# A decoder layer on one core: TensorE's order taken from the source instead of the scheduler, small products gathered into larger groups, and the first norm laid out by hand

## Chip, core and metric

The kernel runs on one core of one Trainium2 chip. The metric is the device time of one execution in microseconds (us), lower is better. The kernel before took 437.94 us, the median of 3 runs (437.6 to 438.55).

## What is computed

One decoder layer for 256 tokens of width 1024 in float32. Cut to what matters:

```python
h = rms_norm(x, norm1_g)
z = h @ w_in                      # RWKV part | MoBA q, k, v | gates of two branches
a = rwkv7_time_mix(shift_mix(z_rwkv))     # 8 heads of 64, a state updated over 256 tokens
b = moba_attention(rope(qk_norm(q)), rope(qk_norm(k)), v)   # 8 heads; one block: causal softmax
m = sigmoid(g_a) * (a @ w_branch_a) + sigmoid(g_b) * (b @ w_branch_b)
x = x + m @ w_out
h = rms_norm(x, norm2_g)
u, g = h @ w_ffn_up               # 2816 channels each
y = x + (gelu(causal_conv3(u)) * g) @ w_ffn_down
```

The RWKV part computes for each head and token the recurrence `S = S * w + (S a) b^T + v k^T`, `y = S r`, then a norm for each head (group norm), a bonus term and a gate. The kernel computes it by 4 chunks of 64 tokens: inside a chunk all tokens are joined by a triangular 64x64 system, whose inverse is built up from 16x16 blocks; between chunks a 64x64 state is passed on.

## The kernel before

**Large products.** Every product with a weight matrix is made in three products of a rounded format, so that nearly float32 remains: both operands are split into a high and a low part, and hh·whi, hl·whi and hh·wlo are summed in PSUM. The weights stream in 125 tiles of 512 KB (128 partitions x 1024). `queue` lists them in the order of use; `load_next` (L228 to L235) issues the next one on SyncE's queue into one of 4 buffers `raw`; `split_hi` (L239) casts it into `whi` on ScalarE (L246; three tiles, the entries of `HI_ENG`, on VectorE); `split_lo` (L251) subtracts on VectorE (L256) and makes `wlo`, of which there are 3 buffers; then the next load is issued, so SyncE's place in the queue hangs on VectorE's. `weights` takes a ready pair and makes the next. `wst` (L273, products 128x256 at L284, L286, L289) and `xst` (L295, products 128x512 at L305, L306, L309) run through one output tile and give control back after each part of a tile.

**Threads.** Between the first projection and branch a, five generators share the engines: `bulk` (the projections k, r, v of RWKV, then q, k, v of MoBA, then 8 gates, then branch b), `chain` (RWKV's chain of small steps), `att` (attention), `gn` (the group norm of each chunk) and `lv1` (the second half of the inverse's upper levels). A thread that yields says what its step costs on TensorE and after what latency the results will be there:

```python
cost, lat = next(th[1])
now_t += cost
th[2] = now_t + lat * SLACK.get(th[0], 1.0)
```

A loop keeps a clock `now_t`, always takes the first thread in the list whose time has come, and stretches the latencies by `SLACK`. So it writes the source's order. The framework's scheduler then orders the instructions of each engine anew by its own estimates, TensorE among them; `tc.issue_after` ties a few places.

**RWKV's chain,** in order: the sigmoids of decay and `a` (L490 ff.); exponentials e2, e3 of the running decay; the norm of kk: sums by small products `pss`, `rq` = 1 / sqrt on VectorE, `rx` = its broadcast on ScalarE, transposed by TensorE (`prx`); then the operands AR and KB (L561 to L579; one KB part on GpSimd at L572, two on VectorE at L574, 64x1024 each). `pgr` (L592) multiplies KB and AR in four groups through two banks of PSUM into G (VectorE, L595). The diagonal 16x16 blocks of G go to DRAM `d1` and come back as `Tb` (SyncE, L602, L604). A solve of 15 steps, two VectorE instructions each (L612, L614), builds their inverses `Xb`, which go out to `d2` and come back as X (L617, L623). Beside this stand the transposes KBt (L634), VU (L647), Z0 (L658), and the bonus and gate products `ch` and `pg` (L675 to L677), read by VectorE at L679 and L685. Then `level` (L704 ff.) uses X: products `pp`, a mask P on VectorE (L708), products `px` and `py`, added into X, for the 16 and the 32 level, half by half. Then the 4 chunks pass one after another: pz, pu (copied into VU on ScalarE and VectorE), pS and py. After each, `group_norm` makes yc and its transposed products `pc`, then yah and yal.

**Attention** (L847 ff.): transposes of q and k, then for each of four quarters (token half, head half) scores `ps`, maximum, exp on ScalarE (L889), normalisation head by head on VectorE, transposes (`ppt`, copied to pT on ScalarE at L905), and the product with v (`po`, into ybh at L917 and ybl at L918).

**Head.** Four loads on SyncE's queue bring x, four more the first weight tiles; norm1_g comes on GpSimd's queue, ten parameter rows (p1) on SyncE's behind the first four weight tiles, the other small parameters on GpSimd's. `norm_t` makes the norm, the transposes and hh, hl (L357, L358) from it. ScalarE loads a function table when the kind of function changes.

**End.** `branch(0)`, then w_out in two halves (xst), after each the transposes `turned` (L1001) with hh (L1004) and hl (L1005) of half of the channels and the squares for the second norm; then 11 rounds of the FFN: `proj2` twice, a convolution and GELU, and `down` (L1043 to L1045) one round later. The token's scale of the second norm is applied after the first product (`token_scale`).

Each PSUM tile is one of three sorts: `acc` (3 banks, for large products), `ch` (3 banks, the chain) and `at` (2 banks, attention).

## Time and profile before

| | |
|---|---|
| median of 3 runs | 437.94 us |
| profiled execution | 438.61 us |
| its span | 436.8 us (1.8 us lie around it) |
| TensorE products, busy in the span | 425.6 us, 3600 instructions |
| VectorE | 301.4 us, 545 |
| ScalarE | 243.0 us, 391 |
| GpSimd | 12.8 us, 21 |
| data moved by DMA | 70.76 MB, mean 162 GB/s |

In the profile PE is TensorE (PEld its weight loads), DVE VectorE, ACT ScalarE, POOL GpSimd and SP SyncE. A group's row gives the line, the engine, the operation, output and inputs by the program's names with their sizes, the number of instructions, the busy time, the mean duration in ns, and the idle time of the engine just ahead with what ended it. A row of the timeline gives the start, the duration, and the same. The duration of a product is longer than the distance between two starts, as products are pipelined.

### The profile page before, as it was taken

What the parts mean: (1) busy time and instruction counts of PE and PEld (TensorE: products, weight loads), DVE (VectorE), ACT (ScalarE), POOL (GpSimd) and SP (SyncE); (2) the same over time, 40 slices, a digit from 0 to 9 for tenths busy, and PEclk for the clock granted to TensorE, in tenths of its full rate; (3) what the DMA queues carried; (4) which work ended last, traced back from release to release, by engine and by line L of the source; (5) the groups of instructions that cost most, each with busy time, mean ns of one, the idle gap of its engine ahead of it and who ended that gap; (6) DMA issues with size and microseconds to landing.
All of it is one profiled execution on the core that took longest, in us unless ns stands there. A gap on an engine that the chain in (4) does not pass through costs nothing.

```text
span 436.8 us, 8837 instructions
## 1 busy us (share of the span) xinstructions
PE 425.6 (97%) x3600; PEld 384.0 (88%) x3600; DVE 301.4 (69%) x545; ACT 243.0 (56%) x391; POOL 12.8 (3%) x21
## 2 busy tenths in 40 slices
PE   7799998999999999999999999999999999999996
PEld 3688996788899989799997899999999999999995
DVE  4695899698456568676796479576576576576573
ACT  6489852644375446777355378455455455465450
POOL 6000040000000000000000000000000000000000
PEclk9999999999999999999999999999999999999999
DMA  8764836543657331164556366655665656565612
GB/s 234 195 190 125 243 94 195 132 129 54 194 154 230 95 104 51 50 190 127 166 182 195 107 211 184 226 189 166 200 192 178 195 193 191 191 182 185 214 50 96
DMA packets 62189, 70.76 MB, mean 162 GB/s; under 512 B 8898, under 2 KB 52617, under 8 KB 62150
## 3 DMA queue, kind: packets, MB, share of 16 engines
q1 hardware_dynamic: 61750, 69.50, 53.1%
q0 software_dynamic: 400, 0.71, 0.6%
q8 instruction: 28, 0.46, 0.4%
q14 instruction: 11, 0.09, 0.1%
HBM read 68.76 MB, written 1.44 MB: 161 GB/s over the span
## 4 chain that ended last, share of the span: by engine, by line
PE 82%; DVE 5%; ACT 5%; DMA 4%; issue 1%; SPq 1%; DVEq 0%; ACTq 0%
PE acc L284 15%; PE acc L286 15%; PE acc L289 15%; PE acc L305 4%; PE f L1045 4%; PE f L1043 4%; PE f L1044 4%; PE acc L306 4%; PE acc L309 4%; DMA raw<-in_w_in_dram 4%; DVE wlo L256 2%; ACT whi L246 1%; PE ps L876 1%; PE pp L704 1%; PE py L720 1%
## 5 line engine op out<-in xcount | busy, mean ns | idle before, releaser
L246 ACT CAST whi<-raw 128x1024 fp32r<-128x1024 f32 x121 | 126.4, 1050 | 119.3 <-PE acc L286 52.6
L256 DVE TENSOR_TENSOR wlo<-raw,whi 128x1024 fp32r<-128x1024 f32 x125 | 152.2, 1219 | 53.1 <-PE acc L289 18.4
L284 PE MATMUL acc<-hh,whi 128*128 128x256 f32 x600 | 150.1, 284 | 1.7 <-ACT whi L246 0.8
L286 PE MATMUL acc<-hl,whi 128*128 128x256 f32 x600 | 148.7, 282 | 0.9 <-DVE hl L358 0.9
L284 PEld LDWEIGHTS acc<-hh,whi 128*128 128x128 f32 x600 | 113.1, 188 | 4.4 <-ACT hh L357 1.5
L286 PEld LDWEIGHTS acc<-hl,whi 128*128 128x128 f32 x600 | 113.1, 188 | 3.2 <-DVE hl L358 1.5
L289 PE MATMUL acc<-hh,wlo 128*128 128x256 f32 x600 | 95.1, 281 | 1.2 <-DVE wlo L256 1.2
L289 PEld LDWEIGHTS acc<-hh,wlo 128*128 128x128 f32 x600 | 80.9, 189 | 2.1 <-DVE wlo L256 2.0
L1044 PE MATMUL f<-whi,hb 128*128 128x512 f32 x80 | 31.1, 389 | 0.0
L1043 PE MATMUL f<-whi,hb 128*128 128x512 f32 x80 | 31.1, 389 | 0.0
L1045 PE MATMUL f<-wlo,hb 128*128 128x512 f32 x80 | 31.1, 389 | 0.0
L305 PE MATMUL acc<-whi,hh 128*128 128x512 f32 x48 | 20.2, 425 | 0.0
L306 PE MATMUL acc<-whi,hl 128*128 128x512 f32 x48 | 18.8, 393 | 0.0
L1058 DVE TENSOR_TENSOR an<-acc,rsb 128x512 f32<-128x512 f32 x11 | 7.6, 691 | 14.8 <-PE acc L289 13.9
L1045 PEld LDWEIGHTS f<-wlo,hb 128*128 128x128 f32 x80 | 15.0, 188 | 3.1
L1044 PEld LDWEIGHTS f<-whi,hb 128*128 128x128 f32 x80 | 15.0, 188 | 2.7
L1043 PEld LDWEIGHTS f<-whi,hb 128*128 128x128 f32 x80 | 15.0, 188 | 2.7
L1076 DVE TENSOR_TENSOR cv<-cv,acc 128x256 f32<-128x256 f32 x22 | 8.3, 418 | 11.5 <-PE acc L289 11.2
L309 PE MATMUL acc<-wlo,hh 128*128 128x512 f32 x48 | 15.0, 393 | 0.0
L1065 ACT ACTIVATE cv<-an,cpar 128x256 f32<-128x256 f32 x22 | 12.0, 594 | 1.4 <-DVE an L1058 0.4
L305 PE MATMUL acc<-whi,mh 128*128 128x512 f32 x32 | 12.8, 399 | 0.0
L306 PE MATMUL acc<-whi,ml 128*128 128x512 f32 x32 | 12.6, 395 | 0.0
(274 smaller groups left out, 566.1 us busy)
## 6 DMA issues: line engine op xcount, KB each, us to landing
raw<-in_w_ffn_up_dram SPq DMA_DIRECT2D x44, 512.0 KB
raw<-in_w_in_dram SPq DMA_DIRECT2D x43, 512.0 KB
raw<-in_w_ffn_down_dram SPq DMA_DIRECT2D x22, 512.0 KB
raw<-in_w_out_dram SPq DMA_DIRECT2D x8, 512.0 KB
x<-in_x_dram SPq DMA_DIRECT2D x8, 256.0 KB
raw<-in_w_branch_b_dram SPq DMA_DIRECT2D x4, 512.0 KB
raw<-in_w_branch_a_dram SPq DMA_DIRECT2D x4, 512.0 KB
out_dram<-o SPq DMA_DIRECT2D x3, 256.0 KB
```

Source lines behind the costliest of these rows:

```text
L246: act.copy(hi[:, :k * c], raw[:, :k * c])
L256: dve.tensor_tensor(lo[:, :n], raw[:, :n], hi[:, :n].bitcast(F32), op=OP.subtract)
L284: pe.matmul(om, wh[:, k, ms], xh[:, k0 + k], start=k0 + k + m == 0, stop=False, skip_group_check=True)
L286: pe.matmul(om, wh[:, k, ms], xl[:, k0 + k], start=False, stop=False, skip_group_check=True)
L289: pe.matmul(om, wl[:, k, ms], xh[:, k0 + k], start=False, stop=k0 + k == nk - 1 and m == n - 1, skip_group_check=True)
L305: pe.matmul(ps_[t], xh[:, K, ts], wh[:, k], start=K == 0, stop=False)
L306: pe.matmul(ps_[t], xl[:, K, ts], wh[:, k], start=False, stop=False)
L309: pe.matmul(ps_[t], xh[:, K, ts], wl[:, k], start=False, stop=K == nk - 1)
L1043: pe.matmul(fin[f], hb[:, 0, i, ts], wh[:, 0, cs], start=st, stop=False)
L1044: pe.matmul(fin[f], hb[:, 1, i, ts], wh[:, 0, cs], start=False, stop=False)
L1045: pe.matmul(fin[f], hb[:, 0, i, ts], wl[:, 0, cs], start=False, stop=False)
L1065: act.activation(cv, pm, AF.Identity, scale=cpar[:, 44 + n:45 + n], bias=cpar[:, 66 + n:67 + n])
```

## The change

- TensorE keeps the source's order (`tc.manual_schedule(engines={PE})`). `SLACK` is gone; the latencies that the threads give are longer, and the costs are set to 0.345 and 0.69 us for a k block. The wait ahead of the upper levels goes from 16.0 (times 1.7) to 11.0.
- Small products come in larger groups: L490 in one group of 8 instead of two, KBt in one and ahead of pgr, pgr in two groups instead of four, over four banks, VU and Z0 in one each, both halves of the upper levels together (`below`, `masked`, `onto`; the thread `lv1` is gone), scores of all eight heads for the first token half, the product with v by token half, normalisation in one multiplication.
- The first norm and the first product are written out in `first_steps`, in which the order of PE, ACT, DVE and POOL is the source's. The first wlo is made on GpSimd. norm1_g, rwkv_mu and the biases come on ScalarE's queue, all other small parameters on SyncE's behind the first four weight tiles; GpSimd loads nothing. The masks are made on GpSimd.
- `HI_ENG` is gone: all casts from the fourth tile on stand on ScalarE.
- q of MoBA is projected ahead of RWKV's v, k and v of MoBA between and after, with the first gate between them.
- At the second norm `turned(0, 4)` stands inside the second half of w_out, `turned(4, 8)` behind the first weight tile of the first FFN product, `token_scale` within the second product.

```diff
-SLACK = {"chain": 1.7, "att": 1.4, "lv1": 2.5, "gn": 2.0}
-        HI_ENG = {i: dve for i in (4, 5, 6)}
...
-        p0 = t1("p0", (8, 128))
-        nc.gpsimd.dma_start(p0, rows(norm1_g, 8))
         x_sb = load_x()
+        load_rows(act, p1, ((rows(norm1_g, 8), 8), (mu1[0:1792].rearrange("(n c) -> n c", c=128), 14),
+                            (mu1[1696:1824].rearrange("(n c) -> n c", c=128), 1),
+                            (rows(decay_bias, 4), 4), (rows(aaa_bias, 4), 4)))
...
         for _ in range(NRAW):
             load_next()
-        for dst, src in p1_loads:
-            nc.sync.dma_start(dst, src)
+        small_loads()
...
+        def first_steps():
...
+            split_hi(dve)
+            split_lo(pool)
+            for k in range(6):
+                parts(k)
+            split_hi(act)
+            parts(6)
+            parts(7)
+            split_lo()
+            split_hi(act)
+            p = acc()
...
+        with tc.manual_schedule(engines={E.PE, E.Activation, E.DVE, E.Pool}):
+            p = first_steps()
+        late_consts()
...
-            yield 0.5, 2.0
+            yield 1.5, 5.0
             dve.tensor_tensor(flat(kp), flat(kp), flat(zk), op=OP.mult)
...
+            yield 1.4, 4.0
+            masks()
+            for g in range(2):
+                pg = [[p.rearrange("p (u i) -> p u i", u=4) for p in pj] for pj in banks("pgr")]
+                for ct in (2 * g, 2 * g + 1):
...
+                yield 2.1, (5.0, 0.1)[g]
...
-                yield 2.6, 0.2
+                yield 2.7, 0.2
...
-            yield 0, 16.0
-            yield from level(0)
-            threads.insert(1, ["lv1", level(1), 0.0])
+            yield 0, 11.0
+            pp = [below(g) for g in range(2)]
+            P = [masked(pp[g], m16) for g in range(2)]
+            yield 2.5, 3.5
+            adds = [onto(0, P[0], 0), onto(1, P[1], 0), onto(0, P[0], 1)]
+            for a in adds:
+                a()
+            yield 3.3, 4.5
...
-                    yield 0, 1.0
+                    yield 0, 6.0
+                    while not joined[0] and "chain" not in done:
+                        yield 0, 0.1
                     p = chp("pc").rearrange("p (a n) -> p a n", a=8)
...
+            p0 = yield from scores(0, 0, 8)
+            yield weighted(0, p0)
+            pa = yield from scores(1, 0, 4)
+            pb = yield from scores(1, 1, 4)
+            yield weighted(1, pa + pb)
+            yield 0, 2.5
             ybs.extend((ybh, ybl))
...
+            rope_tables()
+            yield from attention_input(0)
+            yield from proj4("v", 8)
+            yield from attention_input(1)
+            yield from gates(1, 0)
+            yield from attention_input(2)
+            threads.insert(1, ["att", attention(), now_t + 3.0])
+            for j in range(1, 4):
+                yield from gates(1, j)
+            for j in range(4):
+                yield from gates(0, j)
             while "att" not in done:
                 yield 0, 1.0
             yield from branch(1, *ybs)
...
-                th[2] = now_t + lat * SLACK.get(th[0], 1.0)
+                th[2] = now_t + lat
+                if cost:
+                    joined[0] = th[0] != "bulk"
...
             if j == 0:
-                with tc.issue_after(mid[0]), tc.issue_after(mid[1]):
-                    pa = now(proj2())
-                    token_scale()
+                pa = acc()
+                gen = wst(pa, 2, hh, hl)
+                steps(gen, 2)
+                turned(4, 8)
+                squares(1, *WCUT[1:3])
+                run(gen)
                 fin = [chp("f0"), chp("f1"), chp("f2"), atp("f3")]
+                pb = acc()
+                gen = wst(pb, 2, hh, hl)
+                steps(gen, 2)
+                token_scale()
+                run(gen)
...
     with tile.TileContext(nc) as tc:
-        body(tc, *args)
+
+        with tc.manual_schedule(engines={mybir.EngineType.PE}):
+            body(tc, *args)
```

In the changed text `below(g)` makes the 16 products `pp` of one half, `masked` the mask's multiplication into P, and `onto(g, P, side)` 16 products onto one side of X with the addition handed back as a function; `scores(t, j, nh)` holds what attention did from `ps` to pT for `nh` heads, and `weighted(t, pTs)` the products `po` of one token half; `steps(gen, n)` runs n parts of a product; `squares` makes the sums for the second norm.

More of the change, by code (lines that the diff above doesn't have):

```diff
@@ L395, in body @@
             load_next()
-        for dst, src in p1_loads:
-            nc.sync.dma_start(dst, src)
-        hh, hl, xn, part, first, turn, second = norm_t(x_sb, G1, "1", (0, 512, 1024))
-        for t in range(2):
-            part(t, 0)
-            part(t, 1)
-            if t:
-                with tc.issue_after(last):
-                    last = dve.tensor_copy(par[:, 0:8], pt[:, 0:8]).ins
-                with tc.issue_after(last):
-                    last = first(t)
-            else:
-                last = first(t)
-            turn(t)
@@ L440, in now @@
                     return e.value
-        with tc.issue_after(mid[0]):
-            p = now(proj2())
         xwa = t1("xwa")
@@ new lines, in masked, with onto @@
+            def masked(p, mk):
+                P = b2("P", [128, 8, 64])
+                dve.tensor_tensor(P, p, mk[:, None, :].to_broadcast([128, 8, 64]), op=OP.mult)
+                return P
+            def onto(g, P, side):
+                p, p4 = bank("px")
+                for u, i in us[g]:
+                    for q in range(2):
+                        l, r = X[bsl(q), 1, u], P[bsl(q), i]
+                        if side:
+                            l, r = r, l
+                        pe.matmul(p[bsl(q), i], l, r, start=True, stop=True)
+                return lambda: dve.tensor_tensor(pair(X[:, side], g), pair(X[:, side], g), p4, op=OP.add)
@@ L729, in chain @@
+            yield 2.3, 4.0
             ny = {}
@@ L951, in bulk, with attention_input @@
             yield from proj4("r", 0)
-            yield from proj4("v", 8)
-            for i in range(3):
+            def attention_input(i):
                 qkv.append(b4("qkv", (128, 2, 8, 64)))
@@ L958, in bulk @@
                     finish_qk(ps_[t], i, t)
-            threads.insert(1, ["att", attention(), 0.0])
-            yield from gates(1)
-            yield from gates(0)
+            rope_tables()
[7 more added lines that the diff above has]
+                yield from gates(1, j)
+            for j in range(4):
+                yield from gates(0, j)
             while "att" not in done:
```

513 lines of the change are left out of this document (249 added, 264 removed).

## Prediction

> **What bounds the kernel now.** I read the page first, then the busy time by stretch, then TensorE's timeline around its gaps, then the groups by line.
>
> ```profile
> span 436.8 us, 8837 instructions
> PE 425.6 (97%) x3600; PEld 384.0 (88%) x3600; DVE 301.4 (69%) x545; ACT 243.0 (56%) x391; POOL 12.8 (3%) x21
> PEclk9999999999999999999999999999999999999999
> PE 82%; DVE 5%; ACT 5%; DMA 4%; issue 1%; SPq 1%; DVEq 0%; ACTq 0%
> L246 ACT CAST whi<-raw 128x1024 fp32r<-128x1024 f32 x121 | 126.4, 1050 | 119.3 <-PE acc L286 52.6
> L256 DVE TENSOR_TENSOR wlo<-raw,whi 128x1024 fp32r<-128x1024 f32 x125 | 152.2, 1219 | 53.1 <-PE acc L289 18.4
> ```
>
> TensorE is busy for 425.6 of 436.8 us at the full clock. DVE and ACT have room on the average, but each weight tile costs 1.05 us on ACT and 1.22 on DVE, and every short step of a chain queues behind such an instruction. By stretch (length, then busy time and instructions of PE, its weight loads, DVE, ACT, POOL; clock; DMA share; GB/s):
>
> ```profile
> 0.00:25.60 25.60, 20.25 (x115) 14.62 (x115) 15.98 (x63) 15.47 (x30) 7.84 (x19) 1.00 0.74 205
> 25.60:118.80 93.20, 91.28 (x731) 79.01 (x730) 74.97 (x153) 55.04 (x90) 5.00 (x2) 1.00 0.56 153
> 118.80:224.40 105.60, 105.56 (x1327) 97.51 (x1326) 72.68 (x135) 63.54 (x116) 0.00 (x0) 1.00 0.44 131
> ```
>
> TensorE's gaps are 5.35 us in the head, 1.92 in the second stretch, 0.04 in the third. So the change can win through the head, two stalls, and dead time inside "busy": a switch between large and small products.
>
> ```profile
> 142.56 0.63 PE L289 MATMUL acc<-hh,wlo 128*128 128x256 f32 x4
> 143.11 1.15 PE L704 MATMUL pp<-X,G 64*64 64x64 f32 x32
> 144.19 0.38 PE L284 MATMUL acc<-hh,whi 128*128 128x256 f32 x1
> 144.41 0.28 PE L286 MATMUL acc<-hl,whi 128*128 128x256 f32 x1
> 144.53 0.28 PE L284 MATMUL acc<-hh,whi 128*128 128x256 f32 x1
> ```
>
> The last two starts lie 0.12 apart, the pitch of large products. The fourth L289 starts near 142.91, so L704 comes 0.20 after it: 0.08 lost. The 32 small ones start every 0.03 ((1.15 - 0.22) / 31), the last near 144.04, and L284 follows 0.15 later: 0.12 lost. L286 comes 0.22 after that: 0.10 lost. One visit to small products costs **0.3 us**.
>
> **What is saved.** All large products stay (600 of 128x256 in each of three lines, and so on); I count the same 2496 in both orders. In the order of TensorE's instructions the small ones stand in 55 groups before and 34 after; without the head and the second norm it is 49 and 30. 19 visits x 0.3 = **5.7** (0.2 to 0.35 each: 3.8 to 6.7).
>
> ```profile
> 69.27 0.48 PE L592 MATMUL pgr<-AR,KB 64*128 64x128 f32 x2
> 70.86 1.16 PE L592 MATMUL pgr<-AR,KB 64*128 64x128 f32 x14 [1.10 <-DVE G L595]
> 41.38 0.38 PE L284 MATMUL acc<-hh,whi 128*128 128x256 f32 x1 [0.75 <-ACT whi L246]
> ```
>
> The products of pgr waited for a bank that DVE emptied. In the change they use four banks and come in groups of 32 with 5 us between: 70.86 - 69.27 less two pitches, **1.3**. The wait for a whi at 41.38 falls among groups that are now one: **0.8** (0 to 0.8; the three casts taken from DVE may bring it back, see below).
>
> The head:
>
> ```profile
> 13.68 1.05 ACT L246 CAST whi<-raw 128x1024 fp32r<-128x1024 f32 x1 [2.11 <-DMA raw<-in_w_in_dram]
> 7.60 2.30 SPq L397 DMA_DIRECT2D p<-in_rwkv_mu_dram  x2
> 15.48 0.25 SPq L397 DMA_DIRECT2D p<-in_rwkv_r_k_dram  x1
> 17.93 0.95 SPq L234 DMA_DIRECT2D raw<-in_w_in_dram  x2
> ```
>
> The second raw tile lands late, with POOL's loads beside it, and SP reaches the fifth only at 17.93, behind ten small loads. After, five of them stand on ACT's queue and none on POOL's; but 15 stand on SP behind the fourth raw, the tanh of xwa stands behind two more casts (2.1 us), and the first small group needs it. I take **1.6** saved; the bounds are the whole wait saved (2.1) and 4 lost (15 issues at 0.25 us, as at 15.48). POOL's first wlo lies under the eight hh casts. The masks on POOL (busy 5.00 us in the second stretch) hide under the chain's first products; uncovered they would cost a few tenths. Saved in all: 5.7 + 1.3 + 0.8 + 1.6 = **9.4**.
>
> **What is added.** TensorE now runs strictly as the source says: where the planner's latency is too short, it stands, and nothing can pass. The rows that price it:
>
> ```profile
> 85.38 0.46 SPq L604 DMA_DIRECT2D Tb<-d  x1
> ...
> 100.08 1.49 SPq L617 DMA_DIRECT2D d<-Xb  x2
> 104.02 4.04 SPq L623 DMA_DIRECT2D X<-d  x8
> ```
>
> ```profile
> 77.50 1.29 DVE L595 TENSOR_TENSOR G<-pgr,gmask 128x512 f32<-128x512 f32 x2 [0.99 <-PE pgr L592]
> ...
> 90.44 0.17 DVE L612 TENSOR_TENSOR tmp<-Tb,Xb 128x15 f32<-128x15 f32 x1
> ...
> 94.06 1.23 DVE L256 TENSOR_TENSOR wlo<-raw,whi 128x1024 fp32r<-128x1024 f32 x1 [0.29 <-PE acc L309]
> ...
> 95.86 0.68 DVE L679 TENSOR_TENSOR zr<-ch,zv 128x512 f32<-128x512 f32 x1
> ...
> 99.88 0.17 DVE L614 TENSOR_TENSOR Xb<-Xb,tmp 128x15 f32<-128x15 f32 x1
> ```
>
> ```profile
> 119.73 0.56 PE L704 MATMUL pp<-X,G 64*64 64x64 f32 x10
> ```
>
> ```profile
> L747 ACT ACT_TABLE_LOAD x4 | 5.1, 1283 | 0.1
> L931 ACT ACTIVATE gt<-acc 128x512 f32<-128x512 f32 x8 | 4.8, 594 | 0.1
> L889 ACT ACTIVATE sc<-sc,mx 128x128 f32<-128x128 f32 (+1 forms) x16 | 7.1, 444 | 3.7 <-DVE mx L886 3.7
> L574 DVE TENSOR_TENSOR KB<-kp,L 64x1024 f32<-64x1024 f32 x2 | 4.1, 2068 | 0.0
> L905 ACT COPY pT<-ppt 128x256 f32<-128x256 f32 (+1 forms) x8 | 3.8, 477 | 5.7 <-PE ppt L904 5.5
> L1005 DVE SCALAR_TENSOR_TENSOR hl<-xt,par,hh 128x256 fp32r<-128x256 f32 x8 | 3.5, 479 | 1.3 <-ACT hh L1004 1.3
> L1004 ACT ACTIVATE hh<-xt,par 128x256 fp32r<-128x256 f32 x8 | 3.4, 474 | 7.2 <-PE xt L1001 6.8 <-DVE hl L1005 0.4
> L917 ACT CAST ybh<-po 128x256 fp32r<-128x256 f32 x4 | 1.5, 370 | 2.6 <-PE po L913 2.6
> ```
>
> I went through the changed order of each engine with these durations.
> - The transposes prx need rx. On DVE the two KB products (2.07 each, L574 above) now stand ahead of rq. The planner leaves about 5 us; 4.1 of KB, one wlo and the steps of rq come to 6.3. With a late weight tile behind it: **1.7** (0.4 to 2.5).
> - The second group of ch and pg needs the bank that DVE empties into zr (L679 above). This instruction stands half way through the 30-step solve, which stands behind a wlo that waits for TensorE to free a buffer. In before G ends at 78.8, Tb is issued at 85.38 (6.6 later), the solve starts at 90.44 and zr at 95.86 (5.4 of solve, one wlo within). After, TensorE has 14.6 us of work between the G products and this group (54 large ones of both widths, 11.0, and three small groups, 3.6); DVE has 2.7 of G, then 6.6 to the issue, 3 to the landing (an estimate below the 5.06 from issue to first step in before), 5.4 of solve and at least 0.5 of MoBA's k norm between its steps: 18.2. So **3.6** (0 to 9).
> - The products pp need X. In before X's last issue ends at 108.1; with 1.3 for its landing, an estimate, that is 13.5 behind zr at 95.86, and L704 came only at 119.73: 10 us of room. After, TensorE has 13.7 of work from there (72 large ones, 12.4, and the group itself), and the stretch holds two wlo (2.4) and small steps of the norm more on DVE: **2.6** (0 to 6).
> - pS waits for VU, whose copy stands behind eight exps (0.44 each), a tanh and a cast on ACT: **0.9** (0 to 1.5).
> - The end of attention. In before it ended with 24 large products of the gates left. After, all are gone at the 888th, and then come the last group norm, the last transposes, 16 products po, and branch b, which needs ybh. The norm has a tanh (0.59), a whi (1.05), a table load (1.28) and a sqrt ahead on ACT, the multiplication of sc and a wlo (1.22) on DVE: about 5; then a copy pT (0.48), ybh (0.37) and its remainder: **6.4** (2.4 with nothing queued ahead, to 9).
> - The first FFN product: hh and hl of chunks 4 to 7 are now made after its first raw's products. The first pair takes 0.47 + 0.48, the others follow every 0.47 where the products need one every 0.23: 0.95 + 4 x 0.24 = 1.9, so **2.0** (0.5 to 3.5).
>
> Added in all: 1.7 + 3.6 + 2.6 + 0.9 + 6.4 + 2.0 = **17.2**. Three casts more on ACT (3 x 1.05) I cost at nothing: between 25.6 and 118.8 ACT is busy for 55.0 of 93.2; uncovered they cost 3.2.
>
> **The sum.** 17.2 - 9.4 = +7.8. The profiled execution took 438.61 (span 436.8 and 1.8 around it), so it would become 446.4; against the median of the runs shown, 0.67 lower, **445.7**. With every wait at its low end and the savings as above: 3.3 - 9.4 = -6.1; that end is the first rival.
>
> **The rivals.**
> - *Faster.* The chains do not queue behind casts as I laid them out: waits last only what a chain needs by itself. The solve is the place: if Tb lands early enough that zr and X come in time (0 in place of 6.2), pS 0, prx 0.4, attention's end 2.4, FFN 1.5, the waits are 4.3: 4.3 - 9.4 = -5.1, **432.8**. For it: the planner's latencies are longer and planned for this order, and in before all these chains had room. Against it: DVE's and ACT's order is fixed too, with wlo and whi between the steps. It decides where the waits sum to less than 9.4, 55% of what I found.
> [...]
> - *ACT bounds the second stretch* through the three casts: +3.2, **448.9**.
> - *Gains and waits cancel*: within 0.2%, about what a measurement of this kernel can tell from no change.
>
> **How the numbers follow.** Forecast, waits outweigh gains: 0.48 (its own range 440 to 450). Faster: 0.30 (430 to 437). Clock: 0.10. ACT: 0.07. Cancel: 0.05. So faster 0.30, same 0.05, slower 0.65. The range runs from 431.5, which leaves out a third of the faster case, to 449.5, which leaves out the ends of the slow ones: about 2 in 10.
>
> **What would show it.** Right: fewer switches of 0.3 us; new gaps on PE at the second L678 (line of the changed text) with DVE zr as releaser, at the first pp with X as releaser, and one of 5 us or more ahead of branch b, with PE busy falling well below 97% between 80 and 200 us; in the FFN a wait for hh or hl in the first product, and from there the same time as before. Wrong: no gap over 1 us there, or gaps in other places, a granted clock below 9 after them, or a head that takes longer than 25.6 us to the same product.

## The result, and the profile after

The changed kernel takes 454.62 us (median of 4 runs, 453.51 to 456.9) against 438.01 of before (4 runs): the ratio is 1.0385, with a 95% interval of 1.0343 to 1.0427. The forecast was 445.7, with a range up to 449.5. The direction was right, and the size was half of what came. The profiled execution took 454.87.

The page of the changed kernel, the lines that answer to those of before:

```profile
span 452.9 us, 8818 instructions
PE 425.8 (94%) x3599; PEld 388.6 (86%) x3599; DVE 295.2 (65%) x505; ACT 243.1 (54%) x389; POOL 15.6 (3%) x28
PEclk9969999997969999998999999999999999999999
L243 ACT CAST whi<-raw 128x1024 fp32r<-128x1024 f32 x124 | 130.1, 1050 | 126.2 <-PE acc L283 67.6
L253 DVE TENSOR_TENSOR wlo<-raw,whi 128x1024 fp32r<-128x1024 f32 x124 | 151.0, 1220 | 65.7 <-PE acc L286 27.2
```

TensorE is busy for as long as before (425.8 beside 425.6), though it visits small products less often; its span is 16.1 longer. Two things are to be seen. It stands still for 27.1 us in place of 11.2. And the clock, 9 in every slice before, is 6 or 7 in three slices and 8 in one: a part of the busy time is slow work. By stretch (columns as before: length, then PE, its weight loads, DVE, ACT, POOL; clock; DMA share; GB/s):

```profile
0.00:27.40 27.40, 17.15 (x100) 11.94 (x100) 13.43 (x42) 16.02 (x31) 8.31 (x26) 0.95 0.71 217
...
99.40:140.00 40.60, 33.73 (x279) 29.27 (x280) 23.13 (x68) 12.71 (x18) 0.00 (x0) 0.83 0.44 110
...
209.00:220.00 11.00, 9.62 (x91) 8.76 (x92) 3.28 (x7) 3.07 (x5) 0.00 (x0) 0.84 0.11 37
```

Between 99.4 and 140 TensorE lacks 6.9 us and has 0.83 of its clock; before, no stretch had less than 1.00. TensorE's timeline of the changed kernel, where it waits (the bracket holds the idle time ahead and what ended it):

```profile
27.44 0.87 PE L490 MATMUL at<-xwa,wdu 64*128 64x256 f32 x2 [5.39 <-DMA raw<-in_w_in_dram]
...
107.52 1.22 PE L678 MATMUL pg<-xg,wgu 128*128 128x256 f32 x2 [3.50 <-DVE zr L681]
108.53 1.06 PE L679 MATMUL pg<-xg,wgu 128*128 128x256 f32 x2
...
126.96 0.30 PE L705 MATMUL pp<-X,G 64*64 64x64 f32 x2 [1.70 <-DMA X<-d]
128.93 3.64 PE L705 MATMUL pp<-X,G 64*64 64x64 f32 x62 [1.67 <-DMA X<-d]
...
209.35 1.12 PE L768 MATMUL pc<-ident,yc 64*64 64x64 f32 x16 [4.29 <-DVE yc L761]
...
266.26 0.39 PE L281 MATMUL acc<-hh,whi 128*128 128x256 f32 x1 [0.35 <-ACT hh L1034]
```

Behind the 3.50 two products pg take 1.06 where they took 0.59 before, and behind X 62 products take 3.64 where 32 took 1.15. That is the clock, which the trace has at half (0.50) from 106.85 to 113.68 and from 127.33 to 134.16.

To compare kernels whose small products stand at different places, I take the start of the same large product in each trace, counting large work at 0.116 us for each product 128x256 and 0.232 for each 128x512, about the distance of their starts (0.93 us for 8 of the first from 262.13 on and 1.37 for 6 of the second from 90.36 on, in the changed kernel):

| large work done, us | 10 | 20 | 60 | 70 | 80 | 110 | 120 | 160 | 200 |
|---|---|---|---|---|---|---|---|---|---|
| before, starts at | 27.20 | 38.31 | 100.56 | 110.50 | 122.77 | 177.92 | 200.75 | 243.49 | 284.94 |
| changed, later by | +6.07 | +4.84 | -5.02 | +6.81 | +12.65 | +11.91 | +15.43 | +14.44 | +16.00 |

The change loses 4.8 in the head, wins 9.9 from there to 60, where the groups are larger (by 60, 274 small products are done where before had done 299), loses 17.7 about pg and X, 3.5 at the end of attention (from 110 to 120; 79 and 15 more small products than before are done there), and 1.6 at the second norm. From 200 on, nothing moves.

### The profile page after: what moved, and what is told of

Same layout as the page of the kernel before. It is cut to its first block, busy times and chain, and to the rows that moved or that the text cites. A ratio compares the mean times of both kernels' runs of the same rounds, so it can differ in the third digit from the quotient of the medians.

```text
span 452.9 us, 8818 instructions
## 1 busy us (share of the span) xinstructions
PE 425.8 (94%) x3599; PEld 388.6 (86%) x3599; DVE 295.2 (65%) x505; ACT 243.1 (54%) x389; POOL 15.6 (3%) x28
## 4 chain that ended last, share of the span: by engine, by line
PE 70%; DVE 3%; DMA 3%; ACT 2%; SPq 2%; issue 1%; DVEq 0%; ACTq 0%
PE acc L281 14%; PE acc L283 14%; PE acc L286 14%; PE f L1084 4%; PE f L1085 4%; PE f L1083 4%; PE acc L302 2%; PE acc L303 2%; PE acc L306 2%; PE px L721 1%; PE pp L705 1%; DMA Tb<-d 1%; DMA d<-Xb 1%; SPq L616 1%; PE ppt L912 1%; DVE wlo L253 1%
## 5 line engine op out<-in xcount | busy, mean ns | idle before, releaser
L243 ACT CAST whi<-raw 128x1024 fp32r<-128x1024 f32 x124 | 130.1, 1050 | 126.2 <-PE acc L283 67.6
L281 PE MATMUL acc<-hh,whi 128*128 128x256 f32 x584 | 146.8, 286 | 0.5 <-ACT hh L1034 0.3
L283 PE MATMUL acc<-hl,whi 128*128 128x256 f32 x584 | 143.7, 281 | 0.3
L281 PEld LDWEIGHTS acc<-hh,whi 128*128 128x128 f32 x584 | 110.8, 190 | 3.2 <-ACT hh L1034 0.9
L283 PEld LDWEIGHTS acc<-hl,whi 128*128 128x128 f32 x584 | 110.8, 190 | 1.3 <-DVE hl L1035 0.7
L286 PE MATMUL acc<-hh,wlo 128*128 128x256 f32 x584 | 91.4, 279 | 0.0
L286 PEld LDWEIGHTS acc<-hh,wlo 128*128 128x128 f32 x584 | 78.6, 189 | 0.0
```

Source lines behind the costliest of these rows:

```text
L243: act.copy(hi[:, :k * c], raw[:, :k * c])
L281: pe.matmul(om, wh[:, k, ms], xh[:, k0 + k], start=k0 + k + m == 0, stop=False, skip_group_check=True)
L283: pe.matmul(om, wh[:, k, ms], xl[:, k0 + k], start=False, stop=False, skip_group_check=True)
L286: pe.matmul(om, wl[:, k, ms], xh[:, k0 + k], start=False, stop=k0 + k == nk - 1 and m == n - 1, skip_group_check=True)
```

## The experiments

Each kernel ran beside the kernel before, which took 438.3 to 438.9 in these runs. The gains below are against the changed kernel's 454.62, which was measured in other runs, so a difference of less than 1 us is not read as a gain. My theory after the traces: the strict order makes TensorE stand at four places where an operand is late, and the clock that falls there costs as much again as some of the waits. The rivals are that the latency for X alone is too short, that the new places of the loads do it, and that the operands are late whatever the order.

**The order alone, from both sides.** `e7_no_order` is the changed kernel without the strict order behind the first steps:

```diff
-        with tc.manual_schedule(engines={mybir.EngineType.PE}):
-            body(tc, *args)
+        body(tc, *args)
```

> Only TensorE's order is given back to the scheduler behind the first steps (these stay in the source's order); latencies, groups, loads and all else are as in the changed kernel. In its order the second ch and pg stand apart with 9 large products between them, pp comes 45 to 80 large products later, and at the end ppt comes ahead of pc. Theory A, the strict order is what makes TensorE stand at X and at the end: the waits at pg, X and pc shrink by 3 to 7 in all, the clock stays up there, and 4 to 9 us go (446 to 451). Rival B, the operands are late whatever the order (the solve and the head are not touched): X is waited for at the later place or the gates run out earlier at the end, and under 2 us go (453 or more).

Measured: 440.69, ratio to before 1.0067 (1.0037 to 1.0096): 13.9 us go, more than either theory gave. `e8_before_order` adds the strict order, and nothing else, to the kernel before:

```diff
     with tile.TileContext(nc) as tc:
-        body(tc, *args)
+        with tc.manual_schedule(engines={mybir.EngineType.PE}):
+            body(tc, *args)
```

> The kernel before with one part of the change alone: TensorE in the source's order; its own latencies, groups, loads and queue stay. Its visits to small products go from 55 to 44 without any other edit, worth 3.3 us at 0.3 each. Theory A, the strict order is harmless where the latencies are long (16.0 times 1.7 ahead of X, which leaves 78 us of large products from ch to pp's place): within 3 us of before, 435 to 441. Rival B, the strict order itself costs: the operands of many small steps are late by the planner's clock, and TensorE stands 8 us or more: 446 or more.

Measured: 455.24, ratio 1.0379 (1.0338 to 1.0419). So the strict order costs 14 us in the new text and 17 in the old one; the rest of the change together, which keeps the head as it is, is worth 2 to 3 us in the wrong direction (440.69 beside 438.56 in the same runs). The old text was written for a scheduler that reorders it, and there the order hits another place first: TensorE's timeline of `e8_before_order` shows the parameters' transpose, which the scheduler had put behind a whole tile of large products, standing in front of them. At 20 us of large work this kernel is 4.7 behind before, at 200 it is 15.3 behind.

```profile
17.74 0.32 PE L169 MATMUL pt<-ident,p 51*128 51x51 f32 x1 [8.43 <-DMA p<-in_norm_g_dram]
```

**The head.** In the changed kernel ScalarE's and SyncE's timelines read:

```profile
8.14 1.21 SPq L186 DMA_DIRECT2D wdu<-in_w_decay_up_dram  x1
...
17.83 0.43 SPq L198 DMA_DIRECT2D posi<-in_positions_dram  x1
18.38 26.12 SPq L235 DMA_DIRECT2D raw<-in_w_in_dram  x9
```

```profile
24.57 1.04 ACT L243 CAST whi<-raw 128x1024 fp32r<-128x1024 f32 x1 [4.38 <-DMA raw<-in_w_in_dram]
26.03 1.04 ACT L243 CAST whi<-raw 128x1024 fp32r<-128x1024 f32 x1 [0.42 <-DMA raw<-in_w_in_dram]
26.98 0.41 ACT L445 ACTIVATE xwa<-xwa 64x256 f32<-64x256 f32 x1
```

SyncE needs from 8.14 to 18.26 for the 15 small loads, the fifth weight tile comes behind them, and the tanh that L490 needs stands behind the casts of the fifth and sixth tile. But in the kernel before SyncE reached the fifth tile hardly earlier (17.93 beside 18.38). What is new is the way to the tanh. VectorE stands 2.89 us for the positions, the last of the 15 loads, ahead of the mix that tanh reads, and the two casts ahead of tanh are those that before had on VectorE (through `HI_ENG`). VectorE's timeline of the changed kernel, then ScalarE's of before:

```profile
22.20 0.17 DVE L205 CAST posf<-posi 128x2 f32<-128x2 int32 x1 [2.89 <-DMA posi<-in_positions_dram]
...
24.12 0.47 DVE L427 SCALAR_TENSOR_TENSOR xwa<-acc,par,xwa 128x255 f32<-128x255 f32 x1
```

```profile
23.71 0.42 ACT L447 ACTIVATE xwa<-xwa 64x256 f32<-64x256 f32 x1 [0.81 <-DVE xwa L427]
```

At 9 us of large work the changed kernel is still 1.9 ahead of before (21.55 beside 23.40). `e1_head` moves twelve of the loads:

```diff
         def small_loads():
-            q = nc.sync
-            q.dma_start(wdu[0:64], w_decay_up[0])
-            q.dma_start(wdu[64:128], w_aaa_up[0])
+            q = nc.gpsimd
...
             split_lo(pool)
+            small_loads()
```

> Only the place of twelve small loads is changed: they leave SyncE's queue, where they stand between the fourth and the fifth weight tile, for GpSimd's queue behind the first wlo; three stay on SyncE's. In the changed kernel the fifth tile was issued at 18.38 us and its whi started at 24.57, the first small products L490 at 27.44 after a gap of 5.39. Theory A, SyncE's queue holds the tile: it is issued near 13, L490 starts between 22 and 24, and 3 to 5 us of the total go (about 450 to 451.5). Rival B, ScalarE's order holds L490 (the tanh of xwa behind the casts of two tiles) or GpSimd's loads slow the early tiles as they did before: L490 stays at 26 or later and under 1.5 us go (453 or more). A third: the gain in the head is given back at X, as the chain behind waits for the same transfers: then the total moves less than L490 does.

Measured: 453.35, ratio 1.036 (1.0299 to 1.0422). L490 came at 30.41, later than without the edit (27.44), so this settles nothing. VectorE's timeline shows why. The positions were now issued early on SyncE's queue, and the first step of the rotary tables stood among the hl of the norm and waited for them:

```profile
16.07 0.17 DVE L207 CAST posf<-posi 128x2 f32<-128x2 int32 x1 [5.16 <-DMA posi<-in_positions_dram]
```

`e9_head2` mends that, and takes tanh ahead of the sixth cast:

```diff
+            q.dma_start(posi, positions[0].rearrange("(t p) -> p t", p=128))
...
-        shift(xwa, p[:, 0:256], 12)
-        act.activation(xwa[0:64], xwa[0:64], AF.Tanh)
+        with tc.manual_schedule(engines={E.Activation}):
+            shift(xwa, p[:, 0:256], 12)
+            act.activation(xwa[0:64], xwa[0:64], AF.Tanh)
...
-            rope_tables()
+            with tc.issue_after(xgl):
+                rope_tables()
```

> Again the head alone, with what the first try showed mended: wdu on SyncE's queue, all other small loads on GpSimd's behind the first wlo with the positions first, the rotary tables behind the last of the three mixes on VectorE (in the first try they stood between the hl of the first norm and waited for the positions), and ScalarE's order in this stretch is the source's, so that tanh stands ahead of the cast of the sixth tile. Theory A, the 5.4 us ahead of L490 are SyncE's queue and the casts ahead of tanh: L490 starts between 20.5 and 23.5, the same large product comes 3.5 to 6 us earlier, and 2.5 to 6 us of the total go (448.5 to 452). Rival B, the fifth tile's transfer is late for another reason: the wait moves from L490 to the next large products, and under 1.5 us go.

Measured: 447.7, ratio 1.0195 (1.0162 to 1.0228): 6.9 us go. L490 no longer waits:

```profile
22.05 1.20 PE L494 MATMUL at<-xwa,wdu 64*128 64x256 f32 x8
```

At 20 us of large work this kernel is 1.6 ahead of before, where the changed one is 4.8 behind: the head's loss is the loads on SyncE's queue and the order of ScalarE and VectorE ahead of tanh, together. How much each of them holds was not measured apart.

**pg and X.** VectorE's timeline of the changed kernel, the solve and what stands within:

```profile
100.30 0.17 DVE L626 TENSOR_TENSOR tmp<-Tb,Xb 128x15 f32<-128x15 f32 x1 [2.12 <-DMA Tb<-d]
...
106.78 0.68 DVE L681 TENSOR_TENSOR zr<-ch,zv 128x512 f32<-128x512 f32 x1
...
114.34 1.23 DVE L253 TENSOR_TENSOR wlo<-raw,whi 128x1024 fp32r<-128x1024 f32 x1 [2.28 <-PE acc L286]
...
115.97 0.16 DVE L626 TENSOR_TENSOR tmp<-Tb,Xb 128x15 f32<-128x15 f32 x1
```

It is a ring: pg waits for zr, zr stands in the solve, the solve stands behind a wlo that waits for TensorE to free a buffer, and TensorE waits for pg. `e3_banks` takes pg out of it:

```diff
-                p, pg = chp(), chp("pg")
+                p, pg = (atp("ch"), atp("pg")) if j else (chp(), chp("pg"))
```

> Only the banks of the second group of ch and pg are changed: two banks of the attention sort, which nobody uses at that time, in place of the chain's sort, so this group no longer waits for VectorE's zr. In the changed kernel this wait was 3.50 us, and the products behind it ran at a lower clock (8.17 us for a group that took 2.40). Theory A, X's landing sets the time here and the wait for the bank lies inside the wait for X: the 3.5 us go from this place, the wait for X (3.4 us in two parts) grows by 3 to 6 us, and the total moves by less than 1.5 us (453 to 455). Rival B, the two waits add up: 4 to 6 us go (449 to 451).

Measured: 450.77, ratio 1.0275 (1.025 to 1.03): 3.9 us go, as rival B said (449 to 451) and not my theory A. At 70 us of large work it is 8.2 ahead of the changed kernel, at 80 only 5.0, as X is now waited for longer:

```profile
122.38 0.45 PE L705 MATMUL pp<-X,G 64*64 64x64 f32 x2 [5.30 <-DMA X<-d]
124.28 3.64 PE L705 MATMUL pp<-X,G 64*64 64x64 f32 x62 [1.46 <-DMA X<-d]
```

`e5_pool_solve` puts the 30 steps, the set-up and the copy of Xb on GpSimd:

```diff
-                dve.tensor_tensor(Xb[:, 0, j + 1:16, 0:nn], Xb[:, 0, j + 1:16, 0:nn], tv, op=OP.add)
-            dve.tensor_copy(Xb[:, 1], Xb[:, 0].rearrange("p i n -> p n i"))
+                pool.tensor_tensor(Xb[:, 0, j + 1:16, 0:nn], Xb[:, 0, j + 1:16, 0:nn], tv, op=OP.add)
+            pool.tensor_copy(Xb[:, 1], Xb[:, 0].rearrange("p i n -> p n i"))
```

> Only the engine of the solve is changed: its 15 steps and the set-up and copy of Xb stand on GpSimd, with nothing else between them, in place of VectorE. In the changed kernel the solve took from 100.30 to 116.62 on VectorE (before: 90.44 to 100.05), with MoBA's k norm, wlo and zr between the steps, and X landed near 129. Theory A, X is late because of what stands between the steps on VectorE: GpSimd's steps take 0.3 to 0.4 each, the solve 9 to 12 us from 100, X lands 4 to 7 us earlier, zr no longer waits for the solve, both waits (3.5 and 3.4) shrink below 1 each, and 6 to 10 us go (445 to 449). Rival B, the way through DRAM and SyncE's queue sets X: the waits shrink by under 2 in all, 452 or more. Rival C, GpSimd needs 0.6 or more for a step: no gain, or a loss.

Measured: 447.47, ratio 1.0201 (1.0168 to 1.0233): 7.2 us go. The solve takes 11.7 us (from 100.13 to 111.81) in place of 16.3, and X is there when pp comes; of the two waits only the one for zr stays, now behind MoBA's k norm alone:

```profile
106.70 0.70 PE L678 MATMUL pg<-xg,wgu 128*128 128x256 f32 x2 [2.79 <-DVE zr L681]
108.74 1.06 PE L678 MATMUL pg<-xg,wgu 128*128 128x256 f32 x2
123.07 2.08 PE L705 MATMUL pp<-X,G 64*64 64x64 f32 x64
```

`e10_later` only asks for X later:

```diff
-            yield 0, 11.0
+            yield 0, 17.0
```

> Only one latency is changed: 17.0 in place of 11.0 ahead of the upper levels. In TensorE's order pp comes 48 large products (6 us) later, so the 3.4 us wait for X should go; for this, more of the chain is left when the gates are used up (three chunk steps in place of one behind the 888th large product). Theory A, there is only so much cover, and X's lateness is paid at the end instead: 453 to 460. Rival B, the wait for X is a planning error of its own: 3 to 7 us go (447.5 to 451.5).

Measured: 445.47, ratio 1.016 (1.0118 to 1.0201): 9.2 us go, more than rival B's upper end, although only 3.4 us were waited for X.

```profile
107.09 0.70 PE L678 MATMUL pg<-xg,wgu 128*128 128x256 f32 x2 [3.44 <-DVE zr L681]
107.63 0.59 PE L679 MATMUL pg<-xg,wgu 128*128 128x256 f32 x2
...
128.64 2.08 PE L705 MATMUL pp<-X,G 64*64 64x64 f32 x64
```

In the execution shown the clock stayed up at both places (0.59 and 2.08 for what took 1.06 and 3.64). It was the fastest of the four (443.12, mean granted clock 0.991; the others took 445.31 to 447.87 at 0.980 to 0.985), so how much of the 9.2 is the clock stays open. pp starts at nearly the same time as in the changed kernel (128.64 beside 126.96), with 48 more large products done.

**The clock.** `e4_fill` leaves all work as it is and fills three waits with idle products into a bank that nobody reads:

```diff
+        def fill(n):
+            w = atp("fill")
+            for _ in range(n):
+                pe.matmul(w, ones[:, 0:128], ones, start=True, stop=True)
```

with 14 ahead of the second ch and pg, 14 ahead of pp and 18 ahead of the last pc.

> Nothing of the work is changed; 14 idle products (128x512, bf16, into a bank that nobody reads) are put ahead of the second ch and pg and ahead of pp, and 18 ahead of the last pc: TensorE is busy where it stood in the changed kernel. Theory A, a part of the loss is the clock, which falls in these waits and makes the products behind them slow (the group at 103 took 8.17 with a wait of 3.9, so 1.9 more than its 2.4; pp took about 1.6 more; the end about 2): the granted clock stays at 9 there and 3 to 7 us go (447.5 to 451.5). Rival B, the waits end when their operands come, and what stands behind waits for the next operand anyway: within 1.5 us (453 to 456). If the idle products stand in the way, it is slower by up to 3.

Measured: 448.6, ratio 1.0218 (1.0182 to 1.0254): 6.0 us go by doing more. The page's clock and TensorE's timeline of this kernel:

```profile
PEclk9969999999999999999999999999999999999999
```

```profile
103.40 2.97 PE L118 MATMUL fill<-ones 128*128 128x512 bf16 x13
...
107.48 0.70 PE L686 MATMUL pg<-xg,wgu 128*128 128x256 f32 x2 [0.68 <-DVE zr L689]
108.02 0.59 PE L687 MATMUL pg<-xg,wgu 128*128 128x256 f32 x2
...
126.41 2.04 PE L713 MATMUL pp<-X,G 64*64 64x64 f32 x62 [0.87 <-DMA X<-d]
```

zr comes no earlier (pg at 107.48 beside 107.52), but what stands behind pg runs at full speed. X comes 2.5 us earlier (126.41 beside 128.93), as its chain waits in the ring for TensorE's products. At 70 us of large work this kernel is 3.0 ahead of the changed one, at 80 it is 4.8 and at 120 it is 6.1. So about 6 of the 16.6 us hang on the clock at these three places, through slow products and what waits for them.

Up to 451 us the trace of the changed kernel has the clock at half four times: from 24.93 to 31.76, 106.85 to 113.68, 127.33 to 134.16 and 209.25 to 212.67. The distances between these eight times are 2, 22, 2, 4, 2, 22 and 1 times 3.413 us. In the 3.41 us ahead of the four falls TensorE was busy for 0.53, 0.57, 1.64 and 0.00 us, in the waits of 5.39 ahead of L490, 3.50 for zr, 1.70 for X and 4.29 for yc. How long a wait lasted did not tell whether it cost the clock: behind the 2.79 of `e5_pool_solve` a pair of products pg took up to 1.06, behind the 3.44 of `e10_later` 0.59. What decides between the two was not shown.

**The end of attention.** `e2_end` lets the last pc wait until attention is done:

```diff
                     yield 0, 6.0
+                    if c == 3:
+                        yield from need("att", done)
+                        yield 0, 3.0
```

> Only the order at the end of attention is changed: the last group norm's transposed products pc wait until attention is done, so ppt and po come first and pc falls into branch b. In the changed kernel pc waited 4.29 us for yc, and ppt and po behind it needed only sc, which was ready at 205.7. Theory A, the 4.29 us are the price of pc standing ahead of ppt: TensorE waits at most 1.5 us for sc there, the clock stays at 9, and 4 to 6 us of the total go (449 to 451). Rival B, the end of attention is late by itself, sc and the copies pT and ybh set branch b: under 2 us go (453 or more).

Measured: 453.58, ratio 1.0319 (1.0267 to 1.0372): 1 us, too little to tell from nothing (one of the four executions took 449.31 at a granted clock of 0.992, the others 453.35 to 454.44 at 0.973 to 0.977). The wait for yc was gone, but pT took its place, as ScalarE's order still had the norm's table load and sqrt (1.28 and 0.30) ahead of it, and po ran slow (3.68, beside 1.97 in `e11_end2` below):

```profile
203.42 1.06 PE L915 MATMUL ppt<-ident,sc 128*128 128x128 f32 x8 [0.81 <-DVE sc L906]
206.61 3.68 PE L928 MATMUL po<-pT,qkv 128*64 128x128 f32 x32 [2.13 <-ACT pT L916]
```

`e11_end2` sets the `need` one yield earlier, ahead of the sqrt:

```diff
                     yield 0, 1.0
+                    if c == 3:
+                        yield from need("att", done)
                     dve.tensor_reduce(st[:, 1], sq2, axis=AX.X, op=OP.add)
```

> The end of attention again: the second half of the last group norm (its sqrt with the table load on ScalarE, and pc) stands behind attention's end, so neither pc nor the table load is ahead of ppt, pT and po. The first try moved only pc, and pT then waited behind the sqrt (2.13). Theory A, ScalarE's and TensorE's order is the price: the stop there falls to 1.5 us or less, the clock stays up for po and branch b, and 4 to 6.5 us go against the changed kernel (448 to 450.5). Rival B, sc itself and the copies set the end: under 2.5 us go.

Measured: 449.73, ratio 1.0244 (1.0215 to 1.0273): 4.9 us go.

```profile
204.96 1.06 PE L914 MATMUL ppt<-ident,sc 128*128 128x128 f32 x8 [0.82 <-DVE sc L905]
206.55 1.97 PE L927 MATMUL po<-pT,qkv 128*64 128x128 f32 x32 [0.52 <-ACT pT L915]
```

**The second norm.** `e6_ffn` parts the transposes; `e12_ffn3`, shown here, also holds the squares back until hh is done:

```diff
-                steps(gen, 2)
-                turned(4, 8)
-                squares(1, *WCUT[1:3])
+                steps(gen, 1)
+                turned(4, 6)
+                steps(gen, 1)
+                with tc.issue_after(turned(6, 8)):
+                    squares(1, *WCUT[1:3])
```

> Only the place of the second norm's last transposes is changed: the pair for channel blocks 4 and 5 stands after 12 large products of the first FFN product and the pair for 6 and 7 after 24, in place of all four after 24. In the changed kernel the products behind them waited in steps of 0.4 and cost about 1.9 us, two of them (0.62 in the group and 0.40) for the first pair. Theory A, hh and hl are made while the products run: 0.8 to 1.5 us go (453 to 453.8 beside 454.6). Rival B, ScalarE's squares and cast stand ahead of hh anyway, so the wait only moves: under 0.4.

> On the changed kernel: the transposes for channel blocks 4 to 7 in two pairs behind 12 and 24 large products, and the squares held back on ScalarE until hh is done (in the first try they and a cast stood ahead of hh). Theory A, ScalarE's order is the FFN's 1.5 us: 0.8 to 1.8 go from 160 to 200 us of large products, so 452.8 to 453.8. Rival B, hh's own pace (0.47 against 0.23) is the price: under 0.5.

Measured: 455.32, ratio 1.0382 (1.0367 to 1.0398), and 454.88, ratio 1.0371 (1.0344 to 1.0397): neither gives anything, and from 160 to 200 of large work `e12_ffn3` still loses 1.6 to before. So the squares are not the cause. That hh's own pace is (rival B of the second) is likely but not shown, as in `e12_ffn3` a cast of 1.05 (at 265.97) still stands between the first hh and the others. With the scheduler's order (`e7_no_order`) the loss is not there (21.4 us from 160 to 180 of large work, 21.5 before, 22.8 in the changed kernel); the first starts there lie 0.21 and 0.12 apart where the changed kernel has 0.52:

```profile
255.72 0.37 PE L281 MATMUL acc<-hh,whi 128*128 128x256 f32 x1
255.93 0.28 PE L283 MATMUL acc<-hl,whi 128*128 128x256 f32 x1
256.05 0.65 PE L281 MATMUL acc<-hh,whi 128*128 128x256 f32 x2
```

**Together.** `c1` holds the mended head, the banks, GpSimd's solve and the mended end; `c3` adds the latency 17.0, `c4` the second norm's edit, `c5` gives the order back to the scheduler, `c6` is c3 with Xb and X on GpSimd's queue. `c7` is `e7_no_order` with the mended head and end alone.

> Four edits together on the changed kernel: the mended head, the other banks for the second ch and pg, the solve on GpSimd, the mended end of attention; strict order and the latency 11.0 stay. Theory A, the four places are nearly all that is lost: head 4 to 5, bank and solve 10 to 12 (7.3 by the solve alone, 3.9 by the banks alone), end 4 to 5 go, so 432 to 437, below before's 438 by 0.2 to 1.4%. Rival B, a place that was hidden behind them comes up (X at the strict place of pp, the next tiles in the head): 438 to 444.

> c1 with the latency 17.0 in place of 11.0 ahead of the upper levels. Theory A, the 6 us that c1 waits for X are a planning error: they go, the end takes 1 to 2 back, and the total is 433.5 to 437, faster than before. Rival B, the cover is used up: what goes at X comes back at the end, 438 or more.

> c3 with the FFN's edit: 0.8 to 1.8 less than c3, 432 to 436, if theory A holds for both; c3's own time if the FFN's edit gives nothing.

> c4 with TensorE's order given back to the scheduler behind the first steps. Theory A, with its waits gone the strict order costs nothing any more: within 1.5 us of c4. Rival B, the scheduler still finds work for short waits: 2 to 5 less than c4. Rival C, it tears groups apart and pays switches: 1 to 3 more.

> c3 with the two writes of Xb and the eight loads of X on GpSimd's queue, behind the solve that stands there. Theory A, SyncE's queue held the weight tiles: in c4 the tiles stood still from 95.6 to 117.1 on it, and TensorE waited 3.9 for a whi; this wait goes, X may come up to 3 us later without being waited for (its place has room), and the total is 436 to 439. Rival B, GpSimd's loads take long to issue or land: X is waited for and nothing is won, 441 or more.

> The changed kernel with TensorE's order given back to the scheduler, the mended head and the mended end; solve, banks, latency 11.0 and the FFN as in the changed kernel. Theory A, the four effects are separate: 440.7 for the order alone, 4 to 6 less for the head, 0 to 3 less for the end: 432.5 to 437, faster than before. Rival B, the head's gain is paid back at X, which the scheduler then waits for, as happened in c1: 438 or more.

| kernel | us | ratio to before (95%) |
|---|---|---|
| c1 | 439.78 | 1.0009 (0.9992 to 1.0026) |
| c3 | 441.53 | 1.0068 (1.0047 to 1.009) |
| c4 | 441.52 | 1.0053 (1.0028 to 1.0078) |
| c5 | 442.26 | 1.009 (1.0057 to 1.0122) |
| c6 | 441.0 | 1.0062 (1.0042 to 1.0082) |
| c7 | 435.88 | 0.9952 (0.9932 to 0.9973) |

The single gains did not add up. With the head mended, TensorE is early at pp and waits for X again, in c1 (the execution shown took 442.46, the longest of eleven):

```profile
118.28 0.30 PE L709 MATMUL pp<-X,G 64*64 64x64 f32 x2 [4.10 <-DMA X<-d]
120.48 3.64 PE L709 MATMUL pp<-X,G 64*64 64x64 f32 x62 [1.90 <-DMA X<-d]
```

With 17.0 the wait moves to a weight tile, in c4, since SyncE's queue holds the tiles behind Xb and X:

```profile
112.97 4.04 SPq L641 DMA_DIRECT2D X<-d  x8
117.12 20.52 SPq L237 DMA_DIRECT2D raw<-in_w_in_dram  x9
```

```profile
122.19 0.58 PE L283 MATMUL acc<-hh,whi 128*128 128x256 f32 x1 [3.90 <-ACT whi L245]
```

With X on GpSimd's queue, in c6, the tiles come, but X's loads are issued later (from 115.94 to 120.93; in c4 from 112.97 to 117.01) and X is waited for (rival B):

```profile
122.97 0.44 PE L709 MATMUL pp<-X,G 64*64 64x64 f32 x2 [2.78 <-DMA X<-d]
125.96 3.65 PE L709 MATMUL pp<-X,G 64*64 64x64 f32 x62 [2.54 <-DMA X<-d]
```

c5 against c4 gives no gain for the scheduler there (442.26 and 441.52). c7 beats both kernels, the one before by 0.5% (435.88); its page has

```profile
span 433.7 us, 8829 instructions
PEclk9999999999999999999899999999999999999999
```

It keeps the larger groups, has the head and the end in order, and lets the scheduler carry large products past pp.

## Why the prediction was wrong

The miss is 8.9 us (454.62 - 445.7). Two steps failed: the head, booked as 1.6 saved, where 4.8 were lost; and the clock, kept out of the sum as a rival at a chance of 0.10, where it cost 6.0 at three places. Two of the signs of being wrong that the prediction named came with them: a head longer than 25.6 us to the same product (33.27 in the changed kernel at 10 us of large work, 27.20 before) and a granted clock below 9. Step by step:

- *Fewer visits, 5.7, and the pgr stall, 1.3.* Right in kind and rather small: from 20 to 60 us of large work the change gains 9.9, and both stalls of before are gone there. How much each holds was not measured apart.
- *The head: "I take 1.6 saved".* This step failed in sign: 4.8 were lost. The mechanism that the same paragraph named as a bound (15 issues on SyncE's queue, tanh behind two casts) was the one that acted, as e9_head2 shows (6.9 us of the total). The bound itself was too small: I priced an issue at 0.25 us, but the 15 took 10.1 us (8.14 to 18.26), as the ten of before had taken 10.2 (7.60 to 17.81). That VectorE would stand 2.89 us for the last of them, ahead of tanh, was not in the sum. I took the value nearest to the row that I wanted to see gone, and not to the rows of the queue that the loads were moved into.
- *prx, 1.7, and pS, 0.9.* Neither came. At prx (which starts 0.24 after its large product) the two KB products, priced at 2.07 each, took 1.21 and 1.22. With the head mended (e9_head2) prx starts 0.66 after its large product, so the late head hid 0.4 at most. At pS the rows show no wait.
- *pg, 3.6: measured 3.50. X, 2.6: measured 3.37 in two parts. End of attention, 6.4: 4.29 for yc, and 1.0 for ybh and ybl. First FFN product, 2.0: 1.6 by large work.* Places and releasers were right. The match at pg is luck: from the last pgr to the second group TensorE had 18.4 us of work and not 14.6 (the three small groups took about 7, not 3.6), and VectorE's chain to zr took 21.7 us and not 18.2, of which Tb's landing was 5.3 (95.01 to 100.30) and not 3; the two errors cancel. X likewise came 22.2 us behind zr (106.78 to 128.93), not 16.3 (13.7 of work and 2.6 of wait), but TensorE, with its slow products, came late there too. And pg and X were added up as if each stood alone: they are one ring through VectorE (e3_banks gives back 3.3 of 8.2 at X).
- *The clock, chance 0.10.* It acted: e4_fill gains 6.0 with all work as it was, 3.0 of it at pg. It should have stood in the sum: five of the waits there (1.7, 3.6, 2.6, 6.4 and 2.0) were longer than any that before had behind the head (1.10 at 70.86), so the 9 in all 40 slices of before could not tell what the clock does in such waits. No run shows one figure for what a wait costs by it: slow products stood behind the 2.79 of e5_pool_solve and none behind the 3.44 of e10_later.
- *Faster, 0.30: the chains do not queue as laid out.* It did not come: the computed waits sum to 14.6 (without prx and pS), and 13.8 were there, in part by luck (see pg).
- *ACT bounds the second stretch, 0.07.* No sign: the changed kernel has no wait for a whi in it, where before had one (0.75 at 41.38).

The two failed terms, head (6.4) and clock (6.0), are more than the miss; the savings that were larger and the two waits that did not come stand against them. That split of the remainder is an account and not an experiment.

## What to carry to other kernels

A fixed order on the busiest engine turned late operands into stops: TensorE stood for 27.1 us in place of 11.2. So a planner's latencies must hold the queues of the other engines too: a chain takes the time of its own steps and of all that stands between them (the solve on VectorE 16.3 us in the changed kernel, of which its 30 steps alone are 6). When loads are moved to another queue, look for every engine that waits for the last of them, and take the bound from that queue's own rows. Long waits of TensorE are to be priced with the slow products that can follow them (here 6.0 us at three places), and how much that is can change from one execution to the next (one of e2_end had a mean granted clock of 0.992, the others 0.973 to 0.977). A removed wait is to be followed to the next operand before its gain is counted: four mended places gave 15 us together and not 23.

## What the runs showed of the hardware

- In the changed kernel the granted clock was at half from 106.85 to 113.68 us and from 127.33 to 134.16 (6.83 each), and from 209.25 to 212.67 (3.42). Behind a wait of 2.79 us the pairs of pg took 0.70, 0.86 and then 1.06 (e5_pool_solve); behind one of 3.44 they took 0.70 and then 0.59 (e10_later). With a row of 13 idle products (2.97 us) ahead of pg and another ahead of pp, the second pair behind the first row took 0.59 and 62 products behind the other 2.04 (e4_fill).
- GpSimd took 11.7 us for the 30 steps of the solve, 0.2 to 0.3 us for most of them (e5_pool_solve). On VectorE in before they took 9.6 with other work between them, and 6.2 by themselves (30 of 0.21). For a 128x1024 subtraction GpSimd took 2.37 us where VectorE took 1.22 (the changed kernel).
- One order alone, on one engine, was worth 14 to 17 us of 440 in two different texts, one of them written for a scheduler that reorders it.
